# Ada columns in tiles and on a queue of their own behind marks; x by quarters, c broadcast by TensorE, half of the conv output projection in fp32 unsplit

## The chip, the cores and the metric

The kernel runs on one core of one Trainium2 chip. The metric is device time of one execution in microseconds. A run is also given by its profile: one execution that the hardware profiler recorded. In it PE is TensorE (matmul), DVE is VectorE, ACT is ScalarE, POOL is GpSimd and SP is SyncE, whose queue here does little else than issue DMAs.

## The reference, cut to what matters

Two layers of a decoder trunk on x of 256 tokens and 1024 features, everything in float32. Every sub-layer is modulated by a vector c: `ada_mod` gives shift, scale and gate of 1024 columns each, for two layers with two sub-layers each.

```python
def ada_mod(c, w, b):
    m = jax.nn.silu(c) @ w + b
    shift, scale, gate = jnp.split(m, 3, axis=-1)
    return shift[:, None, :], 1.0 + scale[:, None, :], 1.0 + gate[:, None, :]

def short_conv_mixer(h, w_in, conv_w, w_out):
    S = h.shape[1]
    gb, gc, xv = jnp.split(h @ w_in, 3, axis=-1)
    z = gc * xv
    zp = jnp.pad(z, ((0, 0), (CONV_WIDTH - 1, 0), (0, 0)))
    zc = conv_w[0] * zp[:, 0:S] + conv_w[1] * zp[:, 1:S + 1] + conv_w[2] * zp[:, 2:S + 2]
    return (gb * zc) @ w_out
...
    for i in range(DEPTH):
        shift, scale, gate = ada_mod(c, ada_w[i, 0], ada_b[i, 0])
        h = x * scale + shift
        f = short_conv_mixer(...) if i % 2 == 0 else diff_attention(...)
        x = layer_norm(DEEPNORM_ALPHA * x + gate * f, ln_g[i, 0], ln_b[i, 0])
        shift, scale, gate = ada_mod(c, ada_w[i, 1], ada_b[i, 1])
        h = x * scale + shift
        f = peer_ffn(h, peer_w_q[i], peer_sub_keys[i], peer_u[i], peer_v[i])
        x = layer_norm(DEEPNORM_ALPHA * x + gate * f, ln_g[i, 1], ln_b[i, 1])
```

`peer_ffn` scores 128 x 128 experts by two lists of 128 keys for each of 8 heads, takes the 16 best of each head, and adds `g * gelu(x . u) * v` over them.

## The kernel before, in words

The order is conv mixer (layer 0), norm, PEER block 0 ("peer 0"), norm, attention mixer (layer 1), norm, peer 1, final norm. A weight comes in blocks of 128x1024 float32 (0.5 MB) into a `raw` tile, loaded by SyncE's queue (L69). ScalarE rounds a block to fp32r, which is the high half (L87 in `copy`), VectorE subtracts that from the block, which gives the low half (L90 in `sub`), both into `spt` tiles of the pool `sp` (SPBUFS = 10). TensorE then makes three products, high by high, high by low, low by high. `raw` tiles come in turn from the pool `stream` (STREAM = 6) and, in the mixers, a further pool (12 tiles in conv, 4 in attention).

The ada columns are the 96 blocks of the modulation weights, 128 columns by 1024 each. A block is loaded like a weight, and one VectorE operation (`scalar_tensor_tensor`, L177) multiplies it by `csb`, which is silu(c) broadcast over the partitions (L148, L165), and adds it up over the free axis: one column of 128 sums. 16 of them are needed for the conv mixer's h (`h_first`, L389). The others are a generator `fill` (`units`, `ada_unit`), of which `advance(fill)` takes two columns and `drain(fill)` the rest, as steps among those of the blocks: 24 in the conv mixer, 48 in peer 0, 8 in peer 1. `mod_rows` makes rows of the finished columns by TensorE (L196).

The steps of a block run through `pipeline(steps, 3)`: a step's first half (loads, splits) is issued three steps ahead of its second (products). Within an engine a scheduler sets the order, with `behind` and `issue_after` as extra bounds. The conv mixer's steps are the input projection, then `use` per block of 128 features (gate, z, the three taps into y, y split into yh and yl, L90), then `project_out` (L352: 8 blocks of `w_out`, 3 products of 128x512 for two row tiles and two halves each), then the norm: products by the gate (L266), sums (L268), the normed X (L286), its transposition by TensorE (L207), and from it hh and hl (L213, L214).

In a PEER block the 128 rows of expert keys are taken in three chunks (46, 42, 40). U steps (L141 to L143) make the scores of the experts; gate steps (`G_step`) build two one-hot matrices A and B on VectorE (L825 to L829), multiply them on TensorE (L838) and multiply the result into a ring (L840). V steps (`V_steps`) split a pair of the ring's rows into wh (ScalarE) and wl (VectorE) and multiply them with the two blocks of `peer_v` (L874, 12 products of 128x512 for each block). The last third of V steps follows when the gate steps of the third chunk are done. `late` is the affine of the norm before (L297, X by ln_g and ln_b), issued at the seventh of those last V steps.

Of the kernel before, what the change touches and what calls it, by code (L numbers as in the profile page):

```python
# [20 lines left out]
P = 128  # L21
T = 256
# [15 lines left out]
SPBUFS = 10  # L38
STREAM = 6
# [4 lines left out]
def tile_trunk(ctx: ExitStack, tc: tile.TileContext, x, c, columns, ada_w, ln_g, ln_b, conv_w_in_a, conv_w_in_b,  # L44
# [103 lines left out]
    nc.sync.dma_start(csb, rows_bcast(c[0], D))  # L148
    X = const.tile([P, NT, D], F32, name="X")

# [14 lines left out]
    act.activation(csb, csb, AF.Silu)  # L165
# [13 lines left out]
    def ada_unit(i, s, part):  # L179
# [6 lines left out]
        dve.tensor_tensor(mod[at], a, ada_bT[at], op=ALU.add)  # L186
        yield
# [30 lines left out]
    def ln_params(i, s):  # L218
        gb = raw(), raw()
        sync.dma_start(gb[0], rows_bcast(ln_g[i, s], D))  # L220
        sync.dma_start(gb[1], rows_bcast(ln_b[i, s], D))
        return gb
# [12 lines left out]
    class Norm:  # L235
# [56 lines left out]
        def affine(self, _):  # L292

            gb = ln_params(self.i, self.s)
            for t in range(NT):
                for n, op in enumerate((ALU.mult, ALU.add)):
                    dve.tensor_tensor(X[:, t, :], X[:, t, :], gb[n], op=op)  # L297

# [39 lines left out]
    def project_out(w, yT, accs, engs):  # L338
        def first(q):
            return [load(w[(2 * q + kk) * P:(2 * q + kk + 1) * P, :], engs[kk]) for kk in range(2)]  # L340
# [17 lines left out]
    def conv_mixer(j, hT, cp, fill, prep):  # L358
        gbT = [None] * KC
        gcT = [None] * KC  # L360
        yh = cp.tile([P, KC, T], F32R, name="yh")
        yl = cp.tile([P, KC, T], F32R, name="yl")

        def use(n, ps):
# [9 lines left out]
            y = cp.tile([P, T], F32, tag="y", name="y", bufs=2)  # L374
# [4 lines left out]
            dve.tensor_tensor(y, y, gbT[k], op=ALU.mult)  # L379
            copy(yh[:, k, :], y)  # L380
            last["y"] = sub(dve, yl[:, k, :], y, yh[:, k, :].bitcast(F32))
# [7 lines left out]
        def h_first(q):  # L389
# [3 lines left out]
            if q == 0:  # L393
                sync.dma_start(X, x[0].rearrange("(t p) d -> p t d", p=P))
# [36 lines left out]
        def steps():  # L431
# [16 lines left out]
            yT = [(yh[:, 2 * q:2 * q + 2], yl[:, 2 * q:2 * q + 2]) for q in range(KC // 2)]  # L448
            for st in project_out(conv_w_out[j], yT, acc, SUBS):
                yield st  # L450
                yield advance(fill, 2, ("hT", "y"))
# [5 lines left out]
    def attn_mixer(j, li, hT, ap, prep, late):  # L457
# [145 lines left out]
        def steps():  # L603
# [10 lines left out]
            for h0 in range(0, HEADS, 2):  # L614
# [14 lines left out]
                if h0 == 4:  # L629
                    yield None, late  # L630
# [15 lines left out]
    def peer(i, hT, pp, fill, prep, late):  # L646
# [64 lines left out]

        def topk(t):
# [5 lines left out]
            cand = sp.tile([P, PH, NCAND], F32, tag="sp", name="cand")  # L718
# [298 lines left out]
```

## Time and profile before

| | us |
|---|---|
| median of 3 runs | 1957.65 |
| lowest and highest run | 1955.34, 1959.71 |
| profiled execution, its own time | 1956.54 |
| profiled execution, span | 1954.8 |
| TensorE busy | 1885.1 |
| VectorE busy | 1550.6 |
| ScalarE busy | 905.3 |
| GpSimd busy | 9.5 |

Rows below are of the profiled execution; their times begin at the span's start. In them `[9.39 <-DMA X<-in_x]` behind a row is the engine's idle time ahead of it and what ended it; a wait row gives the total, the number of times, and the longest.

### The profile page before, as it was taken

How to read it: one execution, taken by the hardware profiler on the slowest of the kernel's cores; microseconds unless marked ns; L12 is line 12 of the kernel's file. 1: busy time of each engine (PE TensorE's matmuls, PEld its weight loads, DVE VectorE, ACT ScalarE, POOL GpSimd, SP SyncE). 2: the span in 40 equal slices, each digit the busy share in tenths (PEclk: the TensorE clock that was granted, in tenths of full speed). 3: DMA queues.
4: the chain of work that ended last, by engine and by line, in shares of the span. 5: the costliest groups of instructions: out<-in, count | busy, mean ns of one | idle time of the engine just before them, and what ended most of it. 6: DMA issues, size and time to landing. Idle time of an engine off the chain costs nothing.

```text
span 1954.8 us, 36946 instructions
## 1 busy us (share of the span) xinstructions
PE 1885.1 (96%) x14858; PEld 1720.6 (88%) x14858; DVE 1550.6 (79%) x3138; ACT 905.3 (46%) x1191; POOL 9.5 (0%) x28
## 2 busy tenths in 40 slices
PE   7969999999999999989899899999999999999897
PEld 6969999999999988867798799999999999888786
DVE  7989887887888888876677788878878766888755
ACT  4534555334444444434466545653444444444443
POOL 0000000000000000000100000000000000000000
PEclk9989999999999999999999999999999999999999
DMA  9955655556778765568753246555567555555563
GB/s 383 366 187 159 185 180 177 163 158 210 249 243 256 232 201 173 173 198 279 241 182 111 86 152 184 183 174 161 161 208 226 173 175 181 168 169 181 173 194 97
DMA packets 104412, 378.87 MB, mean 194 GB/s; under 512 B 11568, under 2 KB 12208, under 8 KB 104240
## 3 DMA queue, kind: packets, MB, share of 16 engines
q1 hardware_dynamic: 104096, 376.42, 59.8%
q8 instruction: 116, 1.90, 0.4%
q14 instruction: 56, 0.46, 0.1%
q10 hardware_dynamic: 144, 0.09, 0.0%
HBM read 375.42 MB, written 1.05 MB: 193 GB/s over the span
## 4 chain that ended last, share of the span: by engine, by line
PE 91%; DVE 5%; DMA 2%; issue 1%; ACT 1%; SPq 0%; DVEq 0%; ACTq 0%
PE acc L874 34%; PE ps L141 15%; PE ps L142 15%; PE ps L143 15%; PE ps L838 4%; DVE raw L177 2%; PE acc L352 2%; PE acc L142 2%; PE acc L141 2%; PE acc L143 2%; DVE spt L90 1%; DMA raw<-in_ada_w 1%; DMA X<-in_x 1%; PE ps L517 0%; DMA gsub<-in_attn_subln_g 0%
## 5 line engine op out<-in xcount | busy, mean ns | idle before, releaser
L87 ACT ACTIVATE spt<-raw 128x1024 fp32r<-128x1024 f32 x608 | 641.1, 1058 | 745.3 <-PE ps L142 416.5
L90 DVE TENSOR_TENSOR spt<-raw,spt 128x1024 fp32r<-128x1024 f32 x608 | 741.0, 1222 | 171.3 <-ACT spt L87 166.5
L141 PE MATMUL ps<-hh,spt 128*128 128x256 f32 x2400 | 684.9, 286 | 2.9 <-DVE hh L214 2.4
L142 PE MATMUL ps<-hl,spt 128*128 128x256 f32 x2400 | 681.0, 284 | 0.6 <-DVE hl L90 0.6
L143 PE MATMUL ps<-hh,spt 128*128 128x256 f32 x2400 | 680.5, 284 | 0.0
L874 PE MATMUL acc<-spt,wh 128*128 128x512 f32 x2048 | 565.9, 396 | 4.4 <-ACT wh L87 4.4
L141 PEld LDWEIGHTS ps<-hh,spt 128*128 128x128 f32 x2400 | 460.6, 192 | 6.8 <-issue 3.0
L142 PEld LDWEIGHTS ps<-hl,spt 128*128 128x128 f32 x2400 | 461.4, 192 | 4.0 <-DVE hl L90 0.9
L143 PEld LDWEIGHTS ps<-hh,spt 128*128 128x128 f32 x2400 | 461.3, 192 | 0.0
L874 PEld LDWEIGHTS acc<-spt,wh 128*128 128x128 f32 x2048 | 375.9, 188 | 75.8 <-ACT wh L87 4.6
L874 PE MATMUL acc<-spt,wl 128*128 128x512 f32 x1024 | 319.6, 392 | 3.6 <-DVE wl L90 3.6
L874 PEld LDWEIGHTS acc<-spt,wl 128*128 128x128 f32 x1024 | 191.9, 188 | 44.8 <-DVE wl L90 5.1
L177 DVE SCALAR_TENSOR_TENSOR raw<-raw,csb 128x1024 f32<-128x1024 f32 x96 | 116.1, 1223 | 57.8 <-DMA raw<-in_ada_w 57.7
L87 ACT ACTIVATE wh<-ring 128x512 fp32r<-128x512 f32 x128 | 79.9, 627 | 159.0 <-PE acc L874 148.9
L840 DVE SCALAR_TENSOR_TENSOR ring<-ps,ring 128x368 f32<-128x368 f32 (+2 forms) x192 | 98.1, 512 | 68.6 <-PE ps L838 68.0
L825 DVE TENSOR_TENSOR A<-iota_e,jT 128x1024 f16<-128x1024 f16 x192 | 131.0, 683 | 0.0
L829 DVE TENSOR_TENSOR B<-B,gT 128x368 f16<-128x368 f16 (+2 forms) x384 | 125.1, 334 | 4.0
L90 DVE TENSOR_TENSOR wl<-ring,wh 128x512 fp32r<-128x512 f32 x128 | 88.0, 689 | 38.7 <-ACT wh L87 38.2
L838 PEld LDWEIGHTS <-A 128*128 128x128 f16 x3072 | 91.0, 96 | 31.1 <-issue 14.3
L838 PE MATMUL ps<-B,A 128*128 128x46 f16 (+2 forms) x3072 | 111.7, 182 | 6.6 <-DVE B L829 6.6
L805 ACT ACTIVATE ring<-ps 128x512 f32<-128x512 f32 x128 | 74.7, 584 | 33.8 <-PE ps L143 33.7
L827 DVE TENSOR_TENSOR B<-iota_e,iT 128x368 f16<-128x368 f16 (+2 forms) x192 | 63.4, 331 | 0.0
(204 smaller groups left out, 1179.9 us busy)
## 6 DMA issues: line engine op xcount, KB each, us to landing
raw<-in_peer_u SPq DMA_DIRECT2D x256, 512.0 KB, 3.8
raw<-in_peer_v SPq DMA_DIRECT2D x256, 512.0 KB, 3.9
raw<-in_ada_w SPq DMA_DIRECT2D x96, 512.0 KB, 4.7
raw<-in_peer_w_q SPq DMA_DIRECT2D x32, 512.0 KB, 4.1
raw<-in_attn_w_qk SPq DMA_DIRECT2D x16, 512.0 KB, 4.4
raw<-in_conv_w_in_a SPq DMA_DIRECT2D x12, 512.0 KB, 10.2
raw<-in_conv_w_in_b SPq DMA_DIRECT2D x12, 512.0 KB, 10.2
raw<-in_conv_w_out SPq DMA_DIRECT2D x8, 512.0 KB, 7.2
```

Source lines behind the costliest of these rows:

```text
L87: act.activation(o, i, AF.Copy, scale=scale)
L90: return eng.tensor_tensor(o, a, b, op=ALU.subtract)
L141: pe.matmul(ps, ah, bh, start=first, stop=False)
L142: pe.matmul(ps, ah, bl, start=False, stop=False)
L143: pe.matmul(ps, al, bh, start=False, stop=last)
L177: return lambda: dve.scalar_tensor_tensor(w, w, 1.0, csb, op0=ALU.mult, op1=ALU.mult, accum_out=dst)
L805: act.activation(ring[:, s:s + 2, :].rearrange("p j t -> p (j t)"), st["ps"], AF.Gelu)
L825: dve.tensor_tensor(by_two(A), numbers(0, KEYS), pairs(jT, KEYS), op=ALU.is_equal)
L829: dve.tensor_tensor(by_two(B[:, h]), by_two(B[:, 1]), pairs(gT[:, h], n), op=ALU.mult)
L838: pe.matmul(ps[:, t, :], A[:, t, :], B[:, h, t, :], start=h == 0, stop=h == 1)
L840: dve.scalar_tensor_tensor(r, ps.rearrange("p t j -> p j t"), 1.0 / GSCALE, r, op0=ALU.mult, op1=ALU.mult)
L874: pe.matmul(acc[t][hf], lhs[:, jj, rows], rhs[:, hf * 512:(hf + 1) * 512], start=first and jp == 0 and jj == 0, stop=last and last_pair an ...
```

## The change

- The c vector is loaded as one row of 4 KB on ScalarE's queue; TensorE multiplies a column of ones with it in two fp32 products of 512 columns, and ScalarE's silu reads the result from PSUM in two halves. X is loaded in four quarters of 256 columns, the first on ScalarE's queue, the others on SyncE's, each behind the ada columns of its quarter.
- The ada columns of the PEER blocks go through `single_columns`: tiles `side` of their own (two, in the pool `stream`), loaded by GpSimd's queue, one column per advance, computed one advance after its load is issued, and placed behind `last["mark"]`, which is the gate step's ring product or the V step's `wl`. In the last V steps the columns end ten steps ahead of the end. The affine is a generator as well, with `side` tiles on GpSimd's queue, advanced at the last ten steps.
- STREAM goes from 6 to 5, SPBUFS from 10 to 9; four temporaries of the top-k (cand, f, eq, keys) move out of the pool `sp` into spare space of the ring.
- Blocks 4 to 7 of the conv mixer's output projection are multiplied in plain fp32, neither the weight nor y split: 16 products of 128x512 in place of 48.

```diff
-SPBUFS = 10
-STREAM = 6
+SPBUFS = 9
+STREAM = 5
...
-    nc.sync.dma_start(csb, rows_bcast(c[0], D))
+    crow = raw()[0:1, :]
+    act.dma_start(crow, c)
...
+    def load_x(q):
+
+        cols = slice(q * 256, (q + 1) * 256)
+        (sync if q else act).dma_start(X[:, :, cols], x[0][:, cols].rearrange("(t p) d -> p t d", p=P))
+
+    load_x(0)
...
-    act.activation(csb, csb, AF.Silu)
+    ones = wk.tile([1, P], F32, tag="B", name="ones")
+    pool.memset(ones, 1.0)
+    for hf in range(2):
+        ps, cols = bank(), slice(hf * 512, (hf + 1) * 512)
+        pe.matmul(ps, ones, crow[:, cols], start=True, stop=True)
+        act.activation(csb[:, cols], ps, AF.Silu)
...
+    def side():
+
+        return stream.tile([P, D], F32, tag="side", name="side", bufs=2)
+
+    def single_columns(*which):
+
+        def compute(at, a, n, w):
+            dve.scalar_tensor_tensor(w, w, 1.0, csb, op0=ALU.mult, op1=ALU.mult, accum_out=a[:, n:n + 1])
+            if n == KC - 1:
+                dve.tensor_tensor(mod[at], a, ada_bT[at], op=ALU.add)
+
+        loaded = None
+        for i, s, part in which:
+            a = small.tile([P, KC], F32, tag="ada", name="ada", bufs=2)
+            at = slice(None), 2 * i + s, slice(KC * part, KC * part + KC)
+            for n in range(KC):
+                w = side()
+                pool.dma_start(w, ada_w[i, s, part, n])
+                if loaded:
+                    compute(*loaded)
+                    yield
+                loaded = at, a, n, w
+        compute(*loaded)
         yield
...
         def second(q, parts):
             if q == 0:
                 accs.extend(new_accs())
-            yh, yl = yT[q]
             for t in range(NT):
                 rows = slice(t * P, (t + 1) * P)
-                for kk, (wh, wl) in enumerate(parts):
+                for kk, ws in enumerate(parts):
                     k = 2 * q + kk
-                    for lhs, rhs, first, last in ((yh, wh, True, False), (yh, wl, False, False), (yl, wh, False, True)):
+                    if q >= whole:
+                        products = (yT[q][0], ws[0], True, True),
+                    else:
+                        (yh, yl), (wh, wl) = yT[q], ws
+                        products = (yh, wh, True, False), (yh, wl, False, False), (yl, wh, False, True)
+                    for lhs, rhs, first, last in products:
...
-                if n % 2 == 1:
-                    yield advance(fill)
+                if n % 3 != 0:
+                    yield advance(fill, 1, ("mark",))
...
+            rest = late(side, pool)
             for n, v in enumerate(vs(2)):
                 yield v
-                if n % 3 == 2:
-                    yield advance(fill)
-                if n == 6:
-                    yield None, late
+                if n % 3 != 0 and n < n2 - 10:
+                    yield advance(fill, 1, ("mark",))
+                if n == n2 - 10:
+                    yield drain(fill)
+                    yield advance(rest)
                 if n == n2 - 8:
-                    yield drain(fill)
                     yield None, prep
+                if n in (n2 - 7, n2 - 5):
+                    yield advance(rest, 1, ("mark",))
...
-    fill = units((0, 1, 2), (1, 0, 0), (1, 0, 1), (1, 0, 2), (1, 1, 0), (1, 1, 1))
+    fill = single_columns((0, 1, 2), (1, 0, 0), (1, 0, 1), (1, 0, 2), (1, 1, 0), (1, 1, 1))
...
-        acc = peer(1, hT, pp, units((1, 1, 2)), norm.prepare, late)
+        acc = peer(1, hT, pp, single_columns((1, 1, 2)), norm.prepare, late)
```

On VectorE, at the end of the conv mixer and the beginning of its norm, there stood before, from the last products y by the gate on (`rows` are the gate rows, `acc` the output projection's sums):

```order
L379 TENSOR_TENSOR y<-y,g 128x256 x2
L90 TENSOR_TENSOR spt<-raw,spt 128x1024
L90 TENSOR_TENSOR yl<-y,yh 128x256 x2
L177 SCALAR_TENSOR_TENSOR raw,ada<-raw,csb 128x1024 x10
L266 TENSOR_TENSOR spt<-acc,rows 128x512 x2
L186 TENSOR_TENSOR mod<-ada,smT 128x8
L177 SCALAR_TENSOR_TENSOR raw,ada<-raw,csb 128x1024
L266 TENSOR_TENSOR spt<-acc,rows 128x512
L177 SCALAR_TENSOR_TENSOR raw,ada<-raw,csb 128x1024
L266 TENSOR_TENSOR spt<-acc,rows 128x512
L177 SCALAR_TENSOR_TENSOR raw,ada<-raw,csb 128x1024 x2
L268 SCALAR_TENSOR_TENSOR spt,mv<-X,spt 128x1024
```

In the changed kernel the same place reads (its L434 is the product by the gate, L190 the ada column, L304 and L306 what L266 and L268 were):

```order
L434 TENSOR_TENSOR yf<-yf,g 128x256
L190 SCALAR_TENSOR_TENSOR raw,ada<-raw,csb 128x1024 x7
L199 TENSOR_TENSOR mod<-ada,smT 128x8
L190 SCALAR_TENSOR_TENSOR raw,ada<-raw,csb 128x1024 x5
L304 TENSOR_TENSOR spt<-acc,rows 128x512 x2
L190 SCALAR_TENSOR_TENSOR raw,ada<-raw,csb 128x1024
L306 SCALAR_TENSOR_TENSOR spt,mv<-X,spt 128x1024
L190 SCALAR_TENSOR_TENSOR raw,ada<-raw,csb 128x1024
L304 TENSOR_TENSOR spt<-acc,rows 128x512 x2
L311 TENSOR_SCALAR mv<-mv 128x1
L90 TENSOR_TENSOR spt<-raw,spt 128x1024
```

The subtractions `yl` and `spt` ahead of the columns are gone, twelve columns instead of ten stand ahead of the first gate products, two instead of four among them.

On VectorE, in peer 0, where the gate steps of the third chunk end and the last V steps begin, there stood before (two more ada columns stand eight rows ahead of this piece; the `wl` are those of the V steps that follow):

```order
L829 TENSOR_TENSOR B<-B,gT 128x320
L90 TENSOR_TENSOR spt<-raw,spt 128x1024
L829 TENSOR_TENSOR B<-B,gT 128x320 x2
L177 SCALAR_TENSOR_TENSOR raw,ada<-raw,csb 128x1024
L829 TENSOR_TENSOR B<-B,gT 128x320
L177 SCALAR_TENSOR_TENSOR raw,ada<-raw,csb 128x1024
L840 SCALAR_TENSOR_TENSOR ring<-ps,ring 128x40x8 x2
L90 TENSOR_TENSOR wl<-ring,wh 128x512 x2
L297 TENSOR_TENSOR X<-X,raw 128x1024 x2
```

and in the changed kernel (L890 is L829, L901 is L840, L209 the ada column):

```order
L90 TENSOR_TENSOR spt<-raw,spt 128x1024 x2
L901 SCALAR_TENSOR_TENSOR ring<-ps,ring 128x40x8
L886 TENSOR_TENSOR A<-iota_e,jT 128x1024
L888 TENSOR_TENSOR B<-iota_e,iT 128x320
L890 TENSOR_TENSOR B<-B,gT 128x320 x4
L901 SCALAR_TENSOR_TENSOR ring<-ps,ring 128x40x8 x2
L90 TENSOR_TENSOR wl<-ring,wh 128x512 x2
L90 TENSOR_TENSOR spt<-raw,spt 128x1024 x2
L90 TENSOR_TENSOR wl<-ring,wh 128x512
L209 SCALAR_TENSOR_TENSOR side,ada<-side,csb 128x1024 x2
```

Four ada columns and the affine (L297) have left this place; the first columns stand behind three `wl`.

On GpSimd, whose queue issues the `side` loads now, the changed kernel has from its start on:

```order
L174 MEMSET ones 1x128
L426 MEMSET z 128x2 x2
L219 DMA side<-in_ada_w 128x1024 x2
L426 MEMSET z 128x2 x6
L219 DMA side<-in_ada_w 128x1024 x46
L258 DMA side<-in_ln_g 128x1024
L259 DMA side<-in_ln_b 128x1024
L536 IOTA dist 128x256
```

The first two `side` loads stand behind two rows of memsets only; the others behind the conv mixer's memsets of z, and the attention block's GpSimd operations behind all 48.

## Rows read from the trace of the kernel before

**Rows 1.** Page, busy us, share of the span and instructions:
```profile
PE 1885.1 (96%) x14858; PEld 1720.6 (88%) x14858; DVE 1550.6 (79%) x3138; ACT 905.3 (46%) x1191; POOL 9.5 (0%) x28
```

**Rows 2.** Windows: us, busy PE, PEld, DVE, ACT, POOL, PEclk, DMA share, GB/s:
```profile
6.00:12.00 6.00, 0.00 (x0) 0.00 (x0) 4.91 (x9) 2.07 (x3) 0.00 (x0) 1.00 1.03 419
...
91.00:114.00 23.00, 23.00 (x103) 18.50 (x101) 21.51 (x38) 8.11 (x13) 0.10 (x1) 1.00 0.73 250
...
843.00:866.00 23.00, 15.78 (x116) 12.62 (x115) 17.08 (x28) 5.77 (x8) 0.00 (x0) 0.85 0.67 211
871.00:933.00 62.00, 60.65 (x267) 49.73 (x266) 43.06 (x55) 29.40 (x34) 0.00 (x0) 1.00 0.78 263
```

**Rows 3.** Timeline of all engines at the start: start us, us, what:
```profile
2.04 1.86 PE L415 MATMUL acc<-iota_a,zero 128*128 128x512 f16 x4 [2.04 <-POOL z L372]
...
5.53 1.06 ACT L165 ACTIVATE csb<-csb 128x1024 f32<-128x1024 f32 x1 [3.09 <-DMA csb<-in_c]
...
13.30 1.97 PE L207 MATMUL ps<-ident,X 128*128 128x128 f32 x8 [9.39 <-DMA X<-in_x]
```

**Rows 4.** Timeline of TensorE at the end of the conv mixer:
```profile
113.44 0.62 PE L352 MATMUL acc<-spt,yl 128*128 128x512 f32 x2
127.55 2.82 PE L207 MATMUL ps<-ident,X 128*128 128x128 f32 x12 [13.49 <-DVE X L286]
```

**Rows 5.** Timeline of VectorE at the same place:
```profile
103.33 0.75 DVE L90 TENSOR_TENSOR yl<-y,yh 128x256 fp32r<-128x256 f32 x2
104.00 1.22 DVE L177 SCALAR_TENSOR_TENSOR raw<-raw,csb 128x1024 f32<-128x1024 f32 x1
...
115.45 1.29 DVE L266 TENSOR_TENSOR spt<-acc,rows 128x512 f32<-128x512 f32 x2
...
124.78 1.23 DVE L268 SCALAR_TENSOR_TENSOR spt<-X,spt 128x1024 f32<-128x1024 f32 x1
```

**Rows 6.** Waits of TensorE, 843 to 866: us in total, times, longest:
```profile
PE ps L838 <- DVE B L829: 4.2, 2, 3.0
PE acc L874 <- ACT wh L87: 3.0, 1, 3.0
```

**Rows 7.** Waits of TensorE, 915 to 940:
```profile
PE acc L874 <- DVE wl L90: 2.4, 2, 1.3
```

**Rows 8.** Waits of TensorE, 1822 to 1840:
```profile
PE ps L838 <- DVE B L829: 2.5, 2, 1.3
PE acc L874 <- ACT wh L87: 1.3, 1, 1.3
PE acc L874 <- DVE wl L90: 1.2, 1, 1.2
```

**Rows 9.** Page, costliest groups: busy us, mean ns | idle before, releaser:
```profile
L90 DVE TENSOR_TENSOR spt<-raw,spt 128x1024 fp32r<-128x1024 f32 x608 | 741.0, 1222 | 171.3 <-ACT spt L87 166.5
...
L177 DVE SCALAR_TENSOR_TENSOR raw<-raw,csb 128x1024 f32<-128x1024 f32 x96 | 116.1, 1223 | 57.8 <-DMA raw<-in_ada_w 57.7
```

**Rows 10.** Timeline of TensorE in the attention mixer:
```profile
1074.16 1.16 PE L551 MATMUL ps<-v,aT 128*128 128x128 f32 x8 [1.21 <-ACT aT L87]
1075.25 2.38 PE L517 MATMUL ps<-k,q 64*128 64x128 f32 x16
```

**Rows 11.** Timeline of VectorE, 841 to 862:
```profile
846.30 1.22 DVE L177 SCALAR_TENSOR_TENSOR raw<-raw,csb 128x1024 f32<-128x1024 f32 x1 [1.29 <-DMA raw<-in_ada_w]
...
853.62 1.23 DVE L177 SCALAR_TENSOR_TENSOR raw<-raw,csb 128x1024 f32<-128x1024 f32 x1 [0.64 <-DMA raw<-in_ada_w]
...
856.03 1.23 DVE L177 SCALAR_TENSOR_TENSOR raw<-raw,csb 128x1024 f32<-128x1024 f32 x1 [0.93 <-DMA raw<-in_ada_w]
```

**Rows 12.** Waits of VectorE, 843 to 935:
```profile
DVE raw L177 <- DMA raw<-in_ada_w: 21.8, 11, 3.5
```

**Rows 13.** DMA issues, 871 to 933: count, KB each, median us to landing:
```profile
raw<-in_ada_w SPq DMA_DIRECT2D x12, 512.0 KB, 5.1
```

**Rows 14.** DMA issues, 962 to 967:
```profile
raw<-in_attn_w_qk SPq DMA_DIRECT2D x3, 512.0 KB, 8.0
```

More of the change, by code (lines that the diff above doesn't have):

```diff
@@ L216, in make_hT, with ln_params @@
         return hh, hl
[L218 to L221, printed above, removed]
+    def ln_params(i, s, tile=raw, queue=sync):
+        gb = tile(), tile()
+        queue.dma_start(gb[0], rows_bcast(ln_g[i, s], D))
+        queue.dma_start(gb[1], rows_bcast(ln_b[i, s], D))
         return gb
@@ L290, in norm, with affine @@
             return make_hT(xs, hh, hl, gbc[:, 0], gbc[:, 1])
-        def affine(self, _):
-            gb = ln_params(self.i, self.s)
+        def affine(self, *tiles):
+            gb = ln_params(self.i, self.s, *tiles)
+            yield
             for t in range(NT):
@@ L297, in affine @@
                     dve.tensor_tensor(X[:, t, :], X[:, t, :], gb[n], op=op)
+                yield
     def abank():
@@ L336, in drain, with project_out @@
         return None, second
-    def project_out(w, yT, accs, engs):
+    def project_out(w, yT, accs, engs, whole=KC):
         def first(q):
-            return [load(w[(2 * q + kk) * P:(2 * q + kk + 1) * P, :], engs[kk]) for kk in range(2)]
+            parts = []
+            for kk in range(2):
+                rows = w[(2 * q + kk) * P:(2 * q + kk + 1) * P, :]
+                if q >= whole:
+                    parts.append((raw(),))
+                    sync.dma_start(parts[-1][0], rows)
+                else:
+                    parts.append(load(rows, engs[kk]))
+            return parts
         def second(q, parts):
@@ L360, in conv_mixer @@
         gcT = [None] * KC
-        yh = cp.tile([P, KC, T], F32R, name="yh")
-        yl = cp.tile([P, KC, T], F32R, name="yl")
+        yh = cp.tile([P, KC // 2, T], F32R, name="yh")
+        yl = cp.tile([P, KC // 2, T], F32R, name="yl")
+        yf = cp.tile([P, KC // 2, T], F32, name="yf")
         def use(n, ps):
@@ L373, in use @@
             dve.tensor_tensor(z[:, 2:], ps, gcT[k], op=ALU.mult)
-            y = cp.tile([P, T], F32, tag="y", name="y", bufs=2)
+            half = KC // 2
+            y = yf[:, k - half, :] if k >= half else cp.tile([P, T], F32, tag="y", name="y", bufs=2)
             col = lambda w: smT[:, 160 + 8 * w + k:161 + 8 * w + k]
@@ L378, in use @@
             dve.scalar_tensor_tensor(y, z[:, 0:T], col(0), y, op0=ALU.mult, op1=ALU.add)
-            dve.tensor_tensor(y, y, gbT[k], op=ALU.mult)
+            last["y"] = dve.tensor_tensor(y, y, gbT[k], op=ALU.mult)
+            if k >= half:
+                return
             copy(yh[:, k, :], y)
-            last["y"] = sub(dve, yl[:, k, :], y, yh[:, k, :].bitcast(F32))
+            sub(dve, yl[:, k, :], y, yh[:, k, :].bitcast(F32))
         acc = []
@@ L447, in steps @@
             yield None, prep
-            yT = [(yh[:, 2 * q:2 * q + 2], yl[:, 2 * q:2 * q + 2]) for q in range(KC // 2)]
-            for st in project_out(conv_w_out[j], yT, acc, SUBS):
+            yT = [(yh[:, 2 * q:2 * q + 2], yl[:, 2 * q:2 * q + 2]) for q in range(2)]
+            yT += [(yf[:, 2 * q:2 * q + 2],) for q in range(2)]
+            for st in project_out(conv_w_out[j], yT, acc, SUBS, 2):
                 yield st
@@ L629, in steps @@
                 if h0 == 4:
-                    yield None, late
+                    yield drain(late())
             yield None, prep
@@ L710, in peer @@
         ab = scratch(128).bitcast(F16).rearrange("p (n h k) -> p n h k", n=2, h=PH)
+        cand = scratch(PH * NCAND).rearrange("p (h k) -> p h k", **hk)
+        fs = [scratch(6 * P).rearrange("p (n k) -> p n k", n=6) for _ in range(NT)]
+        eqs, keyss = ([scratch(1024).bitcast(F16).rearrange("p (h k a) -> p h k a", h=PH, k=TOPK) for _ in range(2)]
+                      for _ in range(2))
         def topk(t):
@@ L739, in topk @@
             yield
-            f = sp.tile([P, 6, P], F32, tag="sp", name="f")
+            f = fs[t]
             pos = po.rearrange("t h k -> t (h k)")
```

17 lines of the change are left out of this document (9 added, 8 removed).

## The prediction

> **What bounds the kernel now.** I read the page's busy shares first, then the stages by windows, and for each stage whose TensorE is not full, what it waited for. TensorE is busy 96% of the span [rows 1], so a saving on another engine counts only where TensorE stands still. The change touches five such places. In the first 13.3 us TensorE waits 9.4 us for X [rows 3]. Between the conv mixer's last product (113.44 + 0.62) and the first transposition of the normed X at 127.55 it waits 13.5 us for VectorE [rows 4, 5]. In 843 to 866 it is idle 23.00 - 15.78 = 7.2 us, for B (4.2) and wh (3.0), and the mean granted clock is 0.85, between the two levels of 1.2 and 2.4 GHz, against 1.00 in the V steps behind it [rows 2, 6]. In the last third of peer 0's V steps it loses 2.4 us to wl [rows 7]. At peer 1's passage from the last gate steps to the last V steps it waits 2.5 + 1.3 + 1.2 = 5.0 us [rows 8].
>
> **Prices.** An ada column costs VectorE 1.22 us, 1.15 when several follow each other (115.45 less 104.00 over ten) [rows 5, 9]; the low half of a weight's split costs the same. 0.5 MB on a full DMA system is 1.25 us, at the 419 GB/s of the start [rows 2]. In 91 to 114 TensorE does 96 split products and seven short transpositions in 23.0 us, 0.23 for each product [rows 2]; the 48 that go are worth 11.1 us.
>
> **fp32 products.** The profile has no fp32 product of 128x512. The nearest is L517, also plain fp32: 16 records in 2.38 us, two to a matmul, eight of 128 columns and eight of 256, so 2.38 / (8 x 128 + 8 x 256) = 0.775 ns for a column and record [rows 10]. 512 columns in two records are then 0.79 us, and 16 products 12.7. Bounds: 11.1 (no slower than what goes), and 17.4 at the pace of the L551 row, whose eight records of 128 columns stand 1.09 us ahead of the next row, 0.136 each (0.136 x 4 x 2 x 16) [rows 10]. I take 13.8, a quarter of the way from 12.7 to 17.4, as the fp32 row is short. TensorE's end in the conv mixer moves by +2.7 us.
>
> **Conv tail and norm.** Here VectorE comes last: after the last `yl` at 103.33 it runs ten columns, then the gate products (L266) with four columns between, and the sums of the norm (L268) [rows 5]. The change takes from it, ahead of that run, four `L90 spt` (4 x 1.15) and four `yl` (two took 0.75): 6.1 us. VectorE was busy 21.51 us of the 23 ahead of 114 [rows 2], so nearly all of it shows; I count 5.7, and the run of columns starts at 98.3. Twelve columns then stand ahead of the gate products: 98.3 + 12 x 1.15 = 112.1. The gate products of the first row tile need TensorE's sums, which end at 114.1 + 2.7 = 116.8 for the second tile and four fp32 products (3.4 us) sooner for the first: 113.4. From there by the new order: two gate products 1.2, a column 1.15, L306 1.15, a column 1.15, two gate products 1.2 (the second sum is there by then), `L90 spt` 1.15, L306 1.15, that is 121.6; before, the transposition came 1.5 us after the second L268 ended (124.78 + 1.23 to 127.55), so now at 123.2 instead of 127.55. Gain 4.3 us.
>
> The start shifts all of this. Ahead of the first weights lie 0.5 MB less for c and 0.75 MB less of X, 3.1 us of full DMA; against that GpSimd's queue issues two side columns behind a few memsets, without a wait, 1 MB or 2.5 us. The broadcast c was ready at 5.53 + 1.06 = 6.6 us. Now a row of 4 KB lands no later than c did, two fp32 products of 512 columns follow, at most 2 x 2 x 0.47 by the first L415 row, and half a silu: 6.6 to 8.0 [rows 3]. ScalarE splits the first weight ahead of h, one 1.1 us operation. I take +0.3; bounds -2.5 (most of what is saved in loads) and +1.5 (side columns ahead of everything, c late). Conv and norm: **-4.0 us**, bounds -7 and -1.
>
> **Peer 0's passage** (from the last gate steps to the last V steps). In 843 to 858 VectorE's queue holds four ada columns among the last gate steps, 1.15 each, and waits 1.29 + 0.64 + 0.93 for the loads of three of them [rows 11]: 4 x 1.15 + 2.86 = 7.5 us by which the B products behind them, and then ring and wh, come late. In the new order no column stands there; the first one comes behind three wl. What stays is the chain gate step, B, product, ring, wh: at peer 1's passage, where no column stands, B waits 2.5 and wh 1.3 [rows 8]. I leave 3.5 here. The loss now is 7.2 idle and 0.15 x 23 = 3.5 of low clock, 10.7: **-7.2 us**; bounds -10.7 and -2 (if the clock stays low and the bare chain takes the columns' place).
>
> **V steps of peer 0.** One weight's 12 products of 0.23 take 2.7 us; VectorE has one `L90 spt` for them, half a wl and, in the last third, two thirds of a column: about 2.3. What makes wl late is that it waits 21.8 us for column loads in 11 waits, up to 3.5 each [rows 12]. Now a column is computed one advance after its load is issued, from a tile of its own, behind the wl of its step. **-2.4 us**, bounds -2.4 and 0. The affine products move from step 6 to the last ten steps, which have no columns any more: 0.
>
> **Peer 1's passage.** There the affine of step 6 stands in VectorE's queue ahead of a wl, waiting for its loads; it goes to the end too. wl's 1.2 and some of wh's go: **-1.5 us**, bounds -5.0 and 0.
>
> **At nothing.** One split tile and one stream tile less: in the densest V steps TensorE is busy 60.65 of 62 us [rows 2], so weights are ready in time with ten tiles, and nine still hold four weights. The top-k temporaries leave that pool, which gives back more than is taken. Without this cover a wait of 1 to 3 us a stage would come, as that for B; the upper end has room for it.
>
> Sum: 4.0 + 7.2 + 2.4 + 1.5 = 15.1, so 1956.5 - 15.1 = 1941.4 for a run like the profiled one. That one is 1.1 under the median, so **1942** in the median's terms. The three runs lie 4.4 us apart; 0.2% (4 us) is about what this kernel's times can tell from no change.
>
> **Rivals.**
> *Side loads come late (the other side).* Two tiles in rotation: three V steps (8.2 us) carry two columns, and a load has 8.2 - 1.2 = 6.9 us from its tile's release to its use. Landing took 5.1 in the median in 871 to 933, but 8.0 in the burst of 962 to 967 [rows 13, 14]. VectorE's column then waits, with the next `L90 spt` and wl behind it. At 9.6 us a rotation of two columns is 2.7 us too long; eleven rotations make 29, of which the three weights that nine tiles hold in advance hide 7: +22, and 1942 + 22 = **1964**. It decides from about 9 us. For it: 263 GB/s at a share of 0.78 in these steps [rows 2], and the columns come closer together than before. Against: 5.1 is well under 6.9. The Trainium skill, page "SBUF — State Buffer", section "SBUF: two separate sides", says that descriptors of a load from GpSimd's queue cannot be written while VectorE is in a two-port mode; by that the loads would be later than those from SP, and no run here has shown such a load yet. The Trainium skill, page "DMA: Bandwidth & Descriptors", section "SWDGE vs HWDGE vs iDMA", says that a DMA engine takes the two kinds of queue in turn; by that they would not stand behind the weights' backlog, and 1942 would hold. Chance 0.08.
> *Conv gives nothing.* fp32 products at 17.4, or the side columns ahead of all loads: the first tile's sums come 4 us later, the norm with them, and the 4.0 is gone: **1946**. For it: 419 GB/s at the start leaves no room [rows 2]. Against: VectorE, not TensorE, was last. Chance 0.14.
> *The passage keeps its stall.* The last gate steps have a chain of their own, and the columns only filled VectorE's waits. Then 2 of the 7.2 go, and nothing at peer 1: 1942 + 5.2 + 1.5 = **1949**. For it: wh of [rows 6] waits for the ring, not for a column. Against: three waits for column loads stand in that queue [rows 11]. Chance 0.11.
> *The start gains.* The side loads come behind SP's first loads, and X's first quarter and the weights 2.5 us sooner: 1942 - 2.8 = **1939**. Chance 0.10.
>
> **How the numbers follow.** The forecast has 0.57 and a range of its own of 1938 to 1946. With the rivals from 1939 to 1949 that makes 0.92. All terms at their best give 25.1 us, 1932.5; all at their worst 3 us, 1954.6. The range leaves the outermost two or so on each side out: 1934 to 1952. Slower by over 0.2% is the first rival, 0.08; within 0.2% 0.07, the worst of the second and third cases together; faster 0.85.
>
> **What would show it.** In the new profile: L405's fp32 run in 13 to 14 us; the first normed transposition waits under 10 us; in the passage no column among the gate steps, waits for B and wh of 3 to 4 us in all and a clock near 1.00; side columns in the V steps with waits for DMA of under 1 us; the first conv product at 16 to 18 us. The prediction is wrong if side columns wait in the V steps, if the conv gate products start after 115, or if some 7 us of idle stay in peer 0's passage.

## The result, and the profile after

The changed kernel takes **1976.89 us** in the median of 4 runs (1975.10 to 1979.38), the kernel before 1958.02 beside it: a ratio of 1.0095 [1.0082, 1.0108], 18.9 us slower where 1942 was forecast. The profiled execution took 1977.38 with a span of 1975.6.

The page of the changed kernel, first the busy times (as [rows 1]), then its two groups of V products (L936, which was L874):

```profile
PE 1911.1 (97%) x14846; PEld 1724.5 (87%) x14846; DVE 1542.6 (78%) x3130; ACT 901.5 (46%) x1184; POOL 42.8 (2%) x89
...
L936 PE MATMUL acc<-spt,wh 128*128 128x512 f32 x2048 | 573.7, 401 | 2.5 <-ACT wh L87 2.5
...
L936 PE MATMUL acc<-spt,wl 128*128 128x512 f32 x1024 | 325.9, 398 | 0.0
```

TensorE is busy 26.0 us *longer* than before with no more to do, apart from the fp32 products and the two small products of the ones, and its idle time fell from 69.7 to 64.5 us: taken together, the time was not lost in waits. The V products (the matmuls of the V steps) tell of it: before they took 396 and 392 ns on the average, and now 401 and 398. A stretch of the last V steps without any wait shows it best, 84 us of each kernel (groups by line, TensorE; x is the count). Before, from 1846 to 1930:

```profile
L874 PE MATMUL acc<-spt,wh 128*128 128x512 f32 x248 | 66.3, 389 | 0.0
L874 PE MATMUL acc<-spt,wl 128*128 128x512 f32 x124 | 38.2, 389 | 0.0
```

After, from 1866 to 1950:

```profile
L936 PE MATMUL acc<-spt,wh 128*128 128x512 f32 x243 | 66.4, 395 | 0.0
L936 PE MATMUL acc<-spt,wl 128*128 128x512 f32 x120 | 37.6, 394 | 0.0
```

In 84 us 372 products before, 363 after: 0.226 and 0.231 us each. From start to start the records read 226 to 227 ns before, all alike, and 228 to 241 after, 232 in the middle. 3072 products with 5 to 6 ns more each make 15 to 18 us.

The waits of TensorE in four windows, 100 to 150 us (to be held against [rows 4]), 240 to 270, 843 to 866 (against [rows 6]) and 1050 to 1114:

```profile
PE ps L245 <- DVE mv L311: 5.7, 1, 5.7
...
PE ps L838 <- DVE ring L835: 1.6, 1, 1.6
...
PE ps L899 <- DVE B L890: 2.9, 1, 2.9
PE acc L936 <- ACT wh L87: 1.2, 1, 1.2
...
PE ps L599 <- DVE s L597: 5.8, 1, 5.8
PE acc L405 <- ACT yh L87: 2.3, 3, 1.4
...
```

The conv mixer's norm waits 5.7 us instead of 13.5, and the passage of peer 0 4.1 instead of 7.2. Two waits are new: TensorE stands 1.6 us in the top-k of peer 0 (and again 1.6 in peer 1), and 5.8 us at the end of the attention mixer. Both lie in stages of which the prediction said nothing.

The timeline of the changed kernel at the start (TensorE), then at the conv mixer's end (VectorE, TensorE):

```profile
3.85 3.78 PE L177 MATMUL ps<-raw,ones 1*128 1x512 f32 x4
7.56 1.11 PE L245 MATMUL ps<-ident,X 128*128 128x128 f32 x4
16.98 1.22 PE L479 MATMUL acc<-hh,spt 128*128 128x256 f32 x4 [8.30 <-ACT hh L87]
...
20.11 0.41 PE L483 MATMUL acc<-hh,spt 128*128 128x256 f32 x1
...
23.26 0.28 PE L480 MATMUL acc<-hl,spt 128*128 128x256 f32 x1
...
98.28 1.22 DVE L190 SCALAR_TENSOR_TENSOR raw<-raw,csb 128x1024 f32<-128x1024 f32 x1
...
114.29 0.69 DVE L304 TENSOR_TENSOR spt<-acc,rows 128x512 f32<-128x512 f32 x1 [2.10 <-PE acc L405]
...
104.65 13.89 PE L405 MATMUL acc<-raw,yf 128*128 128x512 f32 x32
124.22 3.67 PE L245 MATMUL ps<-ident,X 128*128 128x128 f32 x16 [5.68 <-DVE mv L311]
```

The fp32 products come as 32 records in 13.89 us, the columns begin at 98.28, and the first normed transposition comes at 124.22. The starts of the stages, from the timelines (us; the columns on the right are experiments, told below):

| first instruction of | before | after | e1 | e4 | e5 |
|---|---|---|---|---|---|
| conv input projection | 16.99 | 16.98 | 16.94 | 16.80 | 16.92 |
| its last product in the first half | 56.05 | 57.94 | 58.57 | 58.38 | 57.88 |
| peer 0, query products | 132.58 | 129.51 | 130.14 | 129.94 | 129.63 |
| peer 0, V products | 460.93 | 462.04 | 461.65 | 459.46 | 456.81 |
| peer 0, last V steps | 858.84 | 860.97 | 855.19 | 853.41 | 850.13 |
| its last V product | 972.25 | 974.66 | 963.90 | 963.76 | 958.84 |
| attention, output products | 1066.32 | 1067.45 | 1057.88 | 1058.01 | 1053.16 |
| last of these | 1100.21 | 1112.66 | 1103.10 | 1091.90 | 1087.06 |
| peer 1, query products | 1110.09 | 1122.55 | 1112.98 | 1102.92 | 1098.07 |
| peer 1, last V product | 1943.49 | 1964.42 | 1946.91 | 1935.98 | 1930.99 |

### The profile page after: what moved, and what is told of

Read it like the earlier page. It is cut to its first block, busy times and chain, and to the rows that moved or that the text cites. A ratio compares the mean times of both kernels' runs of the same rounds, so it can differ in the third digit from the quotient of the medians.

```text
span 1975.6 us, 37060 instructions
## 1 busy us (share of the span) xinstructions
PE 1911.1 (97%) x14846; PEld 1724.5 (87%) x14846; DVE 1542.6 (78%) x3130; ACT 901.5 (46%) x1184; POOL 42.8 (2%) x89
## 4 chain that ended last, share of the span: by engine, by line
PE 93%; DVE 3%; DMA 1%; ACT 1%; issue 1%; DVEq 0%; SPq 0%; ACTq 0%
PE acc L936 36%; PE ps L141 15%; PE ps L142 15%; PE ps L143 15%; PE ps L899 4%; PE acc L405 2%; PE acc L142 1%; PE acc L143 1%; PE acc L141 1%; DVE spt L90 1%; DMA raw<-in_ada_w 1%; PE ps L575 0%; PE acc L480 0%; PE acc L483 0%; DMA gsub<-in_attn_subln_g 0%
## 5 line engine op out<-in xcount | busy, mean ns | idle before, releaser
L936 PE MATMUL acc<-spt,wh 128*128 128x512 f32 x2048 | 573.7, 401 | 2.5 <-ACT wh L87 2.5
L936 PEld LDWEIGHTS acc<-spt,wh 128*128 128x128 f32 x2048 | 378.7, 190 | 82.9 <-ACT wh L87 2.7
L936 PE MATMUL acc<-spt,wl 128*128 128x512 f32 x1024 | 325.9, 398 | 0.0
L936 PEld LDWEIGHTS acc<-spt,wl 128*128 128x128 f32 x1024 | 192.7, 189 | 43.7
L890 DVE TENSOR_TENSOR B<-B,gT 128x368 f16<-128x368 f16 (+2 forms) x384 | 123.8, 333 | 4.6
L899 PE MATMUL ps<-B,A 128*128 128x46 f16 (+2 forms) x3072 | 116.2, 182 | 5.8 <-DVE B L890 5.7
L901 DVE SCALAR_TENSOR_TENSOR ring<-ps,ring 128x368 f32<-128x368 f32 (+2 forms) x192 | 97.4, 507 | 16.7 <-PE ps L899 16.7
L209 DVE SCALAR_TENSOR_TENSOR side<-side,csb 128x1024 f32<-128x1024 f32 x56 | 67.9, 1219 | 6.1 <-DMA side<-in_ada_w 6.0
```

Of the source, the lines that this page charges most:

```text
L209: dve.scalar_tensor_tensor(w, w, 1.0, csb, op0=ALU.mult, op1=ALU.mult, accum_out=a[:, n:n + 1])
L890: dve.tensor_tensor(by_two(B[:, h]), by_two(B[:, 1]), pairs(gT[:, h], n), op=ALU.mult)
L899: pe.matmul(ps[:, t, :], A[:, t, :], B[:, h, t, :], start=h == 0, stop=h == 1)
L901: last["mark"] = dve.scalar_tensor_tensor(r, ps.rearrange("p t j -> p j t"), 1.0 / GSCALE, r, op0=ALU.mult, op1=ALU.mult)
L936: pe.matmul(acc[t][hf], lhs[:, jj, rows], rhs[:, hf * 512:(hf + 1) * 512], start=first and jp == 0 and jj == 0, stop=last and last_pair an ...
```

## The experiments

The runs are called e1 to e12 in the order in which they were made; "the fourth run" and "the fifth run" in the expectations are e4 and e5. Each time stands beside runs of the kernel before on the same chip.

**What slows the V products?** The names in the pool wk, which holds the working tiles wh, wl, A and B of the PEER blocks, tell. In the built program a pool's tiles lie in the order in which their names are first taken. The new column `ones` takes its tile in wk under the name B, and it does so ahead of all others, so B's two buffers (2 x 1472 bytes) come first, and wh and wl move by 2944 bytes: wh from address 113440 to 116384 in a partition. The split tiles, which are the moving operand of the V products, begin at 56096 (after the change at 60192) and lie 4096 bytes apart. 113440 - 56096 is a multiple of 512, and so it was for every slice of wh and wl; 116384 - 60192 is 384 more than one. The shapes of a V product's operands and the PSUM banks that it adds into had not changed. The rival was the odd number of split tiles, or GpSimd's queue. Two runs tell them apart from both sides.

e1, the changed kernel with the other name:

```diff
-    ones = wk.tile([1, P], F32, tag="B", name="ones")
+    ones = wk.tile([1, P], F32, tag="wh", name="ones")
```

> The changed kernel with one word changed: the column of ones takes its place in the wk pool under the name wh instead of B, so that wh, wl, A and B lie at the addresses that they had before the change (wh at 113440 instead of 116384). Theory 'address': the V products (128x512) run at 227 ns again instead of 232, which over 3072 of them gives 13 to 16 us back: 1961 to 1964. Rival 'nine tiles': the slower products come from the odd number of split tiles or from GpSimd's queue, and the time stays at 1977 with 232 ns.

Measured: 1960.69 us, ratio to before 1.0009 [1.0000, 1.0019], 16.2 us under the changed kernel. From 1860 to 1944:

```profile
L936 PE MATMUL acc<-spt,wh 128*128 128x512 f32 x248 | 66.6, 389 | 0.0
L936 PE MATMUL acc<-spt,wl 128*128 128x512 f32 x125 | 38.7, 389 | 0.0
```

373 products in 84 us, as before the change. From the first V product to the last, peer 0 takes 10.4 us less than in the changed kernel and peer 1 9.4 us less. One word in a line that allocates half a kilobyte costs 16.2 us.

e2, the kernel before with the unused column:

```diff
+    ones = wk.tile([1, P], F32, tag="B", name="ones")
+    pool.memset(ones, 1.0)
     act.activation(csb, csb, AF.Silu)
```

> The kernel before with nothing but an unused column of ones that takes a B tile first in the wk pool, which shifts wh and wl by 2944 bytes. Theory 'address': V products at 232 ns and 12 to 16 us more: 1970 to 1974. Rival 'nine tiles': 1958, V products at 227 ns.

Measured: 1970.05 us, 1.0065 [1.0048, 1.0082]. From 1860 to 1944:

```profile
L876 PE MATMUL acc<-spt,wh 128*128 128x512 f32 x243 | 66.4, 395 | 0.0
L876 PE MATMUL acc<-spt,wl 128*128 128x512 f32 x120 | 37.6, 395 | 0.0
```

363 products, 11.0 us more: the place of the tiles alone does it, in a kernel with ten split tiles and no load on GpSimd's queue. From the first V product to the last it is 7.1 us more in peer 0 and 6.8 in peer 1; 1.4 of them come back ahead of peer 0's first V product, and why was not tried.

**Is it the address or the distance?** e7 moves all tiles by 64 bytes, e8 only wk and the pools behind it, against the split tiles:

```diff
     const = ctx.enter_context(tc.tile_pool(name="const", bufs=1))
+    pad = const.tile([P, 16], F32, name="pad")
+    nc.gpsimd.memset(pad, 0.0)
```

and

```diff
+    pad = ctx.enter_context(tc.tile_pool(name="pad", bufs=1)).tile([P, 16], F32, name="pad")
+    nc.gpsimd.memset(pad, 0.0)
     wk = ctx.enter_context(tc.tile_pool(name="wk", bufs=2))
```

> The kernel before with 64 bytes of padding ahead of all pools' tiles, so that split tiles, hh, wh and wl all move by 64 bytes together. Theory 'relative': the pace of the V products hangs on the distance of the stationary tile (wh, wl) to the moving one (split tile), which stays, so 227 ns and about 1958. Rival 'absolute': it hangs on the address of wh itself, so that the pace may change to 232 ns, 1970.

> The kernel before with 64 bytes of padding ahead of the wk pool alone: wh and wl move by 64 bytes against the split tiles. Theory 'relative': V products slow down, 229 to 233 ns, 1964 to 1972. Rival 'coarse': 64 bytes are less than the step at which it changes, 227 ns and 1958.

Measured in one run each: 1957.66 and 1971.63 us. e7, from 1846 to 1930:

```profile
L876 PE MATMUL acc<-spt,wh 128*128 128x512 f32 x248 | 66.4, 389 | 0.0
L876 PE MATMUL acc<-spt,wl 128*128 128x512 f32 x124 | 38.1, 389 | 0.0
```

e8, from 1860 to 1944:

```profile
L876 PE MATMUL acc<-spt,wh 128*128 128x512 f32 x242 | 66.4, 396 | 0.0
L876 PE MATMUL acc<-spt,wl 128*128 128x512 f32 x120 | 37.7, 396 | 0.0
```

With the same distance 372 products, with 64 bytes more 362. It is the distance. e8 moved the conv and attention mixers' yh and yl too, which its expectation leaves out; what came of that stands in the last section.

**Nine split tiles.** e3 is the kernel before with one edit:

```diff
-SPBUFS = 10
+SPBUFS = 9
```

> The kernel before with SPBUFS 9 instead of 10 and nothing else. Theory 'order': the attention mixer's end is planned in another order (output products ahead of the last scores), which costs some 5.7 us there; V products stay at 227 ns: 1962 to 1965. Rival 'nine tiles': all V products at 232 ns, 1972 or more. Rival 'nothing': 1958.

Measured: 1973.21 us, 1.0076 [1.0059, 1.0092]; V products at 227 ns. The loss is where 'order' put it, but larger: from the first to the last output product of the attention mixer it takes 50.5 us instead of 33.9. In this stage TensorE waits 11.2 us, where before it waited 2.6 (1.7 for aT and 0.9 for yh). The two longest of its waits from 1040 to 1125, but for that of the norm behind:

```profile
PE ps L541 <- DVE s L539: 5.7, 1, 5.7
...
PE ps L572 <- DVE o L570: 1.6, 1, 1.6
```

Three rows of TensorE there with ten tiles (one set of scores L517, the first output products L352, and the transposition L541 of the softmax of these scores; other rows left out):

```profile
1064.11 0.70 PE L517 MATMUL ps<-k,q 64*128 64x256 f32 x4
...
1066.32 1.09 PE L352 MATMUL acc<-spt,yh 128*128 128x512 f32 x4
...
1072.35 0.60 PE L541 MATMUL ps<-ident,s 128*128 128x128 f32 x4
```

and with nine:

```profile
1067.08 1.09 PE L352 MATMUL acc<-spt,yh 128*128 128x512 f32 x4
...
1073.35 0.70 PE L517 MATMUL ps<-k,q 64*128 64x256 f32 x4
...
1082.01 1.09 PE L541 MATMUL ps<-ident,s 128*128 128x128 f32 x4 [5.75 <-DVE s L539]
```

With ten tiles 24 output products stand between these scores and that transposition. The scheduler, with a tile less, issues 18 of them ahead of the scores and leaves 6; when VectorE and ScalarE then make the softmax, TensorE has too little left to cover it. VectorE, for its part, had stood waiting for the scores and not for a split tile: its longest wait from 1064 to 1084 with nine tiles, and the same wait from 1058 to 1073 with ten:

```profile
DVE s L521 <- PE ps L517: 4.9, 1, 4.9
...
DVE s L521 <- PE ps L517: 0.5, 1, 0.5
```

No weight is late: no wait of TensorE in this stage names a split tile. The waits are 8.6 of the 16.6 us. Much of the rest is the clock: over this stage the granted clock is 1.00 before, and here it falls behind the long wait and again at the end (0.66 from 1109 to 1114). Behind the long wait (a window, columns as in [rows 2]):

```profile
1082.00:1089.00 7.00, 6.31 (x28) 4.91 (x28) 2.60 (x11) 1.53 (x7) 0.00 (x0) 0.50 0.06 24
```

The eight records of the values' products behind that transposition (L551) take 2.07 us, before 1.16, and the sixteen of the next scores 3.32, before 2.38.

e4, from e1, gives the tile back and takes one stream tile for it:

```diff
-SPBUFS = 9
-STREAM = 5
+SPBUFS = 10
+STREAM = 4
```

> The changed kernel with the ones at wh and SPBUFS back at 10, STREAM at 4 to make room. Theory 'order': against the first run of this call the attention mixer's end gives 5 to 6 us back, so 1956 to 1958, if four stream tiles are enough; V products at 227 ns. Rival: four stream tiles make the U or V steps wait for loads, 1962 or more.

Measured: 1950.98 us, 0.9964 [0.9953, 0.9976], 9.7 under e1. The attention mixer's output products take 33.9 us again, and its end shows the waits of before. Four stream tiles suffice. Two numbers changed at once here, so the 9.7 us are those of the pair; e3 has the split tile by itself.

**The top-k's temporaries.** e5, from e4, has them in split tiles again, as before the change:

```diff
-        cand = scratch(PH * NCAND).rearrange("p (h k) -> p h k", **hk)
-        fs = [scratch(6 * P).rearrange("p (n k) -> p n k", n=6) for _ in range(NT)]
...
+            cand = sp.tile([P, PH, NCAND], F32, tag="sp", name="cand")
...
-            f = fs[t]
+            f = sp.tile([P, 6, P], F32, tag="sp", name="f")
...
-                eq, keys = eqs[n], keyss[n]
+                eq = sp.tile(shape, F16, tag="sp", name="eq")
...
+                keys = sp.tile(shape, F16, tag="sp", name="keys")
```

> The fourth run (changed kernel, ones at wh, ten split tiles, four stream tiles) with the temporaries of the top-k back in the split tiles. Theory 'scratch waits': the single cand and eq/keys buffers in the ring make the second row tile's top-k wait, and TensorE waits for the ring (L838 from L835) in both PEER blocks, 1 to 1.8 us each; without them the fourth run gains 1 to 3.5 us: 1947.5 to 1950. Rival 'no matter': within 1 us of the fourth run, 1950 to 1952.

Measured: 1945.89 us (1940.95 to 1949.51), 0.9927 [0.9905, 0.9949], 5.1 under e4. No wait of TensorE is left from 220 to 280 and from 1200 to 1280. That the buffers in the ring are too few is the likely reason; it was not tried by itself. In e4 these waits are 0.9 us in each PEER block, so 1.8 of the 5.1 us are accounted for. For the rest the clock is a candidate: in peer 0's passage e4's profiled execution has a mean granted clock of 0.84 (841 to 863) and e5's 1.00 (838 to 860), with the same waits of TensorE (2.4 us for B, 1.3 for wh), and 0.16 of 22 us are 3.5 us. Over the four runs of e5 the time goes with the mean granted clock, from 1940.95 us at 0.992 to 1949.51 at 0.987. The size of this term is therefore uncertain by some microseconds.

**The start.** e6, from e4, has c and X loaded as before:

```diff
-    crow = raw()[0:1, :]
-    act.dma_start(crow, c)
+    nc.sync.dma_start(csb, rows_bcast(c[0], D))
...
-            if q:
-                load_x(q)
+            if q == 0:
+                sync.dma_start(X, x[0].rearrange("(t p) d -> p t d", p=P))
```

> The fourth run with the start of the kernel before: c broadcast by one load of 0.5 MB, X in one load, no ones. Theory 'cold start': after the new start TensorE's first conv products go at half their pace (256 columns in 0.21 us until about 22 us) since it idled ahead of them, and the silu comes 1.7 us later, so that the input projection ends some 2.5 us late; the old start gives 2 to 3 us back: 1948 to 1949. Rival 'the loads pay': the smaller loads are worth 1 to 2 us, and the time rises to 1952 to 1953.

Measured: 1949.95 us, 0.9942 [0.9925, 0.9959]: not clearly other than e4. Neither theory is borne out in the trace, where two effects cancel: the first half of the input projection ends at 58.85, in e4 at 58.38. Its timeline of TensorE:

```profile
16.04 1.97 PE L237 MATMUL ps<-ident,X 128*128 128x128 f32 x8 [12.12 <-DMA X<-in_x]
...
19.87 0.58 PE L471 MATMUL acc<-hh,spt 128*128 128x256 f32 x1 [0.16 <-ACT spt L87]
```

With the old loads, but GpSimd's two side loads among them, X comes at 16.04 instead of 13.30 and the first product at 19.87 instead of 16.99: 1 MB of side loads among the first loads most likely costs these 2.9 us. The new start wins 3.1 of that back (16.80 in e4), and loses 2.6, mostly by its pace, from there to the end of the first half (41.6 us in e4, 39.0 in e6).

e10, from e5, holds the side loads back:

```diff
                 w = side()
+                if (i, s, part, n) == (0, 1, 2, 0):
+                    pool.tensor_copy(w[:, 0:1], mod[:, 1, 0:1])
                 pool.dma_start(w, ada_w[i, s, part, n])
```

> The fifth run with GpSimd's first two side loads held back until the shift and scale of peer 0 are there: a copy of one column into the side tile, which the load then overwrites, waits for them. Theory 'collision': at the start 1 MB less lies among the first loads, the first conv weight lands some 2.5 us sooner and so does the end of the input projection: 1943 to 1944. Rival 'cold': TensorE starts sooner but at half its pace, or silu and h come last, and under 1 us is left: 1945 to 1946.

Measured: 1946.86 us, 0.9935 [0.9920, 0.9951]; 'cold' is the nearer one. Its timeline of TensorE:

```profile
18.27 1.23 PE L481 MATMUL acc<-hh,spt 128*128 128x256 f32 x4 [9.37 <-ACT hh L87]
...
21.43 0.41 PE L481 MATMUL acc<-hh,spt 128*128 128x256 f32 x1
```

The end of the first half of the input projection comes at 57.03 instead of 57.88; the first product still waits for hh and comes at 18.27, later than e5's 16.92.

**The other output products.** e9, from e5, puts yh, yl and yf at the distance that wh and wl have:

```diff
+        pool.memset(cp.tile([P, 96], F32, name="pad"), 0.0)
         yh = cp.tile([P, KC // 2, T], F32R, name="yh")
...
+            if h0 == t == 0:
+                pool.memset(ap.tile([P, 120], F32, name="pad"), 0.0)
             o, rs = os[h0]
```

> The fifth run (changed kernel with ones at wh, ten split tiles, four stream tiles, top-k in split tiles) with padding that puts yh, yl and yf of the conv mixer and yh, yl of the attention mixer at the same place modulo 512 bytes as the split tiles, as wh and wl are. Theory 'relative': the split output products go from 232 to 227 ns there as well: 48 and 96 of them at 5 ns, under 1 us in all, about 1945. Rival 'only wk': they stay at 232 ns.

Measured: 1947.14 us, 0.9940 [0.9925, 0.9956], no different from e5. The mechanism is there, however. The products with yh from 88 to 104, in e5:

```profile
L405 PE MATMUL acc<-spt,yh 128*128 128x512 f32 x28 | 7.9, 398 | 0.0
```

and in e9:

```profile
L405 PE MATMUL acc<-spt,yh 128*128 128x512 f32 x29 | 8.1, 393 | 0.0
```

5 ns less; from start to start 232 became 227. On 144 products that is 0.7 us, under what the runs resolve.

e11 has the edits of e9 and e10.

> Both edits of the two runs ahead of this one in one kernel. If they add up: 1942 to 1943, that is 0.8 to 0.9% under the kernel before. If neither does anything: 1946.

Measured: 1949.82 us (1944.71 to 1950.99), 0.9953 [0.9939, 0.9966]: they don't add up to anything.

**The queue.** e12, from e5, has the side loads on SyncE's queue:

```diff
-                pool.dma_start(w, ada_w[i, s, part, n])
+                sync.dma_start(w, ada_w[i, s, part, n])
...
-            rest = late(side, pool)
+            rest = late(side, sync)
```

> The fifth run with the side loads on SyncE's queue, where the weights' loads stand, instead of GpSimd's. Theory 'own tiles do it': what frees the last V steps and the passage is the two tiles and the place behind the marks, and the queue is of no matter: 1944 to 1948. Rival 'own queue does it': a side load whose tile is not free yet holds up the weights behind it in SyncE's queue, and weights come late: 1950 or more.

Measured: 1943.63 us, 0.9921 [0.9905, 0.9936]. VectorE's wait for side loads from 850 to 960 is the same; e5 first:

```profile
DVE side L209 <- DMA side<-in_ada_w: 5.8, 8, 1.6
```

and e12:

```profile
DVE side L209 <- DMA side<-in_ada_w: 6.1, 7, 2.6
```

The queue is of no matter. That leaves the tiles of their own and the place behind the marks; neither was tried by itself. e12 and e5 are the two quickest versions, 0.8 and 0.7% under the kernel before.

## Why the prediction was wrong

The forecast was 15.1 us faster, and the kernel is 18.9 slower. The step that failed is **At nothing**: "One split tile and one stream tile less", "The top-k temporaries leave that pool, which gives back more than is taken", and, not named there at all, the column of ones, which the text took for a term of the start alone. With these three undone, one after the other, the time falls from 1976.9 to 1960.7, 1951.0 and 1945.9: 16.2 + 9.7 + 5.1 = 31.0 us. The last of these is the least certain, since e5's runs lie 8.6 us apart. What stands then, 0.73% under the kernel before or 14.3 us, is close to the sum that the prediction made (15.1); that it is so close is in part luck, as the points below show terms that miss on either side. Two of the three were put on the kernel before as well, and cost 11.0 (e2) and 14.2 (e3) there.

The reasoning behind "nothing" looked at the resource only: nine tiles still hold four weights, and that was right, since no wait of TensorE behind the start names a split tile. It did not look at what a smaller pool does to the order that the scheduler makes, and the order could have been read ahead: the rows of TensorE in the attention mixer were there to compare, and I compared the places at which the change was aimed. The address of a tile was not thought of at all.

Point by point, by the terms of the sum:

- *fp32 products*: 13.8 taken, 13.89 measured. The quarter of the way from 12.7 to the upper bound was a guess that came out well; 512 columns in two records are 0.87 us, not 0.79.
- *Conv tail and norm*: columns from 98.28 (98.3), gate products from 114.29 (113.4, they wait for TensorE), transposition at 124.22 (123.2). Right as times, with some luck: the 98.3 was reckoned without the later start of the next point (1.9 us), and that does not show in it.
- *The start*: +0.3 taken, +1.9 measured at the end of the first half of the input projection, though the first product comes at the same time. The two products of the ones took 3.78 us (the row of L177 above) and not at most 1.9, so that silu ended at 8.26 instead of 6.59, past the 8.0 that I had as the latest; but the first product waits for hh, and comes no later for it. The pace behind it is what counts. The row of 20.11 above shows it: 256 columns in 0.41 us, starts 0.21 apart, until 22.9, and 0.28 and 0.12 from then on. Before, the same products ran at the quick pace from 18.6 on. TensorE had worked from 13.3 on before, on transpositions and two products with zeros; now it does its transpositions at 7.6 and stands idle for 8.3 us. Conv and norm in all: -3.1 instead of -4.0.
- *Peer 0's passage and V steps*: from the first V product to the last, 511.3 us before, 502.0 in e5: -9.3 against -9.6 in the sum. The split between the two was off: -4.6 (of 7.2) up to the last V steps, -4.7 (of 2.4) in them. The low clock of the passage, which I had counted as gone, stays. In the changed kernel:

```profile
853.00:862.00 9.00, 4.88 (x69) 4.29 (x65) 6.17 (x15) 3.31 (x5) 0.00 (x0) 0.65 0.33 113
871.00:933.00 62.00, 62.00 (x268) 50.27 (x267) 50.89 (x68) 29.11 (x33) 7.93 (x15) 1.00 0.89 309
```

  (windows, columns as in [rows 2]). Granted clock 0.65 in the 9 us of the passage; in the profiled executions of e1 and e5 it is 1.00 there, in e4 0.84, so these differences hold the clock of the one execution as well. In the last V steps TensorE is full and VectorE busy 50.9 of 62 us instead of 43.1.
- *Peer 1's passage*: -1.5; from its first query product to its last V product 833.4 us before, 832.9 in e5, and 830.9 in e10 and 830.8 in e12. About right.
- Not foreseen: the norm behind peer 0 takes 7.1 us from the last V product to the transposition in the changed kernel, and 6.3 in e5, instead of 4.7. In VectorE's queue two small operations on constants of the attention mixer stand ahead of the norm's first gate product, and wait for their loads. That gate product starts 2.4 us ahead of the last V product before (969.87), 0.8 ahead in e5 (958.02), and together with it in the changed kernel (974.67), which accounts for the whole of it; no run has these loads earlier.

The rival that I had put on the other side, side loads that come late, fell. Landing in 871 to 933 and the wait of VectorE for them from 855 to 960, in the changed kernel:

```profile
side<-in_ada_w POOLq DMA_DIRECT2D x15, 512.0 KB, 5.3
...
DVE side L209 <- DMA side<-in_ada_w: 6.0, 5, 2.8
```

VectorE does wait for them, 6.0 us, where the prediction had under 1 and took a wait for a sign of being wrong. But they land in 5.3 us, less than the 5.7 of the weights in the same stretch, and no wait of TensorE stands behind it: from 866 to 974 it has none. The Trainium skill, page "SBUF — State Buffer", section "SBUF: two separate sides", says that VectorE in a two-port mode keeps descriptors of such loads from being written; the trace shows no such delay here, with VectorE busy 82% and loads that land in 5.3 us. No row tells whether VectorE was in such a mode, so this does not test that rule. Slower it was, at a chance of 0.08 that I gave to this mechanism and to no other.

## What to carry to other kernels

A change that adds a tile can move the addresses of others: where TensorE is the bound, compare the pace of its commonest product before and after (start to start, to the nanosecond) before looking for waits. A smaller pool may cost nothing as a resource and still change the order that a scheduler makes: read the orders against each other over the whole program, on the engine that is the bound, and in the stages that the change isn't about. Edits that are "at nothing" deserve a run of their own.

## What the runs showed of the hardware that was not expected

The pace of a product of 128x512 in fp32r hangs on the distance of its stationary and its moving tile in a partition, here given modulo 512 bytes: at 0 it is 226 to 228 ns from start to start (V products before, e1, e7; conv output products in e9; 229 in the mean in the attention mixer of e9), at 384 it is 232 (after, e2), at 64 it is 233 (e8), at 128 it is 232 (conv output products before), and at 32 it is 233 in the mean (attention output products before). e8 adds two: 192, with 229 (its conv output products), and 96, with 234 in the mean (its attention output products). So a distance other than 0 need not cost the whole difference. Only these seven distances were seen; 256 is not among them, and as 128 and 384 give the same pace, the period may be shorter than 512. Products of 256 columns had the distance 0 in all runs and take 120. What inside the chip makes the difference is not shown.

After an idle stretch of 8 us at the start TensorE's first products ran at half their pace for some 6 us, while the granted clock of these windows reads 1.00, so the column does not tell of it there:

```profile
18.00:24.00 6.00, 5.11 (x28) 4.92 (x28) 5.22 (x10) 1.46 (x2) 0.00 (x0) 1.00 1.04 402
```

28 products in 6 us, where the kernel before had 49:

```profile
18.00:24.00 6.00, 6.00 (x49) 5.90 (x50) 6.00 (x10) 1.06 (x1) 0.00 (x0) 1.00 1.03 410
```
